# Encoder trunk: weight-block sums moved from the vector engine to accumulating DMAs, and the last norm spread into the last product's own PSUM bank

## Chip, cores and metric

The kernel runs on one core of one Trainium2 chip. The metric is the device time of one execution in microseconds (us). Before the change three runs gave a median of 1677.84 us (1677.39 to 1680.4). Matrix products run on TensorE (PE in the profile), elementwise work on VectorE (DVE) and ScalarE (ACT); GpSimd (POOL) and SyncE (SP) mostly issue DMAs.

## The reference

One layer of an encoder, 1024 positions by 1024 channels, in float32. Only its second part matters here:

```python
merged = jnp.einsum('blkd,blkd->bld', gates, proj)
x = x + g1 * (merged @ w_out[l])
h2 = rmsnorm(x, norm2_g[l]) * (1.0 + sc2) + sh2
f = jnp.square(jax.nn.relu(h2 @ w_ff1[l])) @ w_ff2[l]      # d_ff = 4096
x = x + g2 * f
return rmsnorm(x, final_g)
```

`w_out` is 1024x1024; `w_ff1` (1024x4096) and `w_ff2` (4096x1024) are used as four 1024x1024 blocks each.

## The kernel before

Everything up to `merged` is the first phase and ends near 930 us of the profile; the change touches `phase2` only.

**Products.** `phase2` multiplies nine pairs of 1024x1024 matrices, one per stage. Stage 0 is `w_out` (eight plain products of 512x512 quadrants). Stages 1 to 8 are the four pairs `w_ff1` block, `w_ff2` block, and use a scheme with seven products of quadrant sums instead of eight (`PW`, `PX`, `WSUM`, `XSUM`): the weight operands of a stage are the quadrants 11, 12, 21, 22 and the four sums S1 = 21+22, S2 = S1+11, S3 = 11+21, S4 = S2+12. Each sum exists for two halves h (128 partitions x 1024 float32, 512 KB), so there are 8 stages x 4 sums x 2 halves = 64 of them. Stages with an odd number ("nl", input h2) and an even one ("lin", input f) take the products in different orders; stage 1 has an order of its own, stage 8 the order `EDGE`.

**Granules.** One half of one product is a granule, numbered J = 0 to 127: granules 0 to 15 are stage 0, 16 to 29 stage 1, 30 to 43 stage 2, and so on in steps of 14; 114 to 127 are stage 8. A granule is 24 matmuls of 128x512. Float32 operands are split into a high and a low part: `w2_split(J)` makes `whi` (ACT) and then `wlo` (DVE) from the raw block, `x2_split(J)` makes `xhi` (ACT) and `xlo` (DVE). Weight operands and x operands have four slots each, J modulo 4.

**Order of the work.** The loop over G issues, for each granule: the matmuls of G (with `take(n)` at the start of a product, which reads the previous product out of its four PSUM banks), then `w2_loads(G + 8)` (SP loads raw blocks into eleven raw tiles as these come free), `w2_add(J)` for the sums of the next granules, `w2_split(G + 3)`, the x splits up to G + 3, and `x2_load(G + 3)`. Each engine executes its instructions in that written order and waits in it. In stage 1 the x operands (h2) are also stored to DRAM by POOL (`hop<-xhi`, `hop<-xlo`, two per granule, line 1539), and in all later "nl" stages POOL loads them from there (line 1546). In stage 0 `take_out(i)` updates x and POOL stores it (`xsp`, line 1597).

**Sums.** `w2_add(J)` (line 1447) makes each sum that granule J needs with one DVE addition, `self.add(dst, f[a], f[b])`, once both inputs have their tiles and, where a quadrant's tile is overwritten (`at`), once that quadrant has been split. The loop calls it for J up to G + 4, and in some iterations (lines 1768 to 1770) also for G + 5 to G + 8, after the splits.

**The norm of h2.** `columns(1, ..)` in the middle of granule 17 reduces the squares, `spread(banks[0][0])` in the middle of granule 18 lets PE broadcast the row factors into a PSUM bank, and ACT copies them into `rb` (`nrm<-pm`); `normed` and the splits of granules 20 to 23 follow at the end of granule 18 (line 1719). Bank 0 of that set is free for the spread once ACT has copied the previous product into `u` (`take(0)`).

**The end.** The last product (granules 126 and 127) is computed in two column halves q = 0, 1 of 256. Ahead of it stand `take(54)` (DVE updates, ACT squares), and `scaled` (eight ACT copies); after its first quarter come `spread(banks[0][0])`, which needs a bank that `take(54)` still reads, and `final` (four POOL multiplications by `rb`). `summed()` lets PE add up squares; `take_part(q)` updates x from half q; `rows_part(q)` computes the row factors on DVE (with one ACT square root), `spread_part(q)` broadcasts them, and `last` multiplies and stores the output.

Of the kernel before, what the change touches and what calls it, by code (L numbers as in the profile page):

```python
# [44 lines left out]
class Program:  # L45
# [1401 lines left out]
    def w2_add(self, J):  # L1447


        s, pos, h = self.gran[J]  # L1450
        f = self.wform.get((s, h), {})
        for n, st in enumerate((self.wplan[s][pos] or ((),))[0]):
            if st[0] == "sum" and (J, n) not in self.wdone:
                _, name, a, b, at, freed = st
                if not {a, b, at or name} <= f.keys() or {at, freed} & {self.wplan[s][q][1] for q in range(pos)
                                                                     if (s, q, h) not in self.wsplit}:
                    return False
                self.wdone.add((J, n))
                dst = f[at or name]
                self.add(dst, f[a], f[b])  # L1460
                f[name] = dst
                if freed:
                    self.rawfree.append(f[freed])
        return True
# [83 lines left out]
    def phase2(self):  # L1548
# [50 lines left out]
        def take(n):  # L1599
            s, pos = divmod(n, 7)  # L1600
            s += 1
            kind, order = self.STAGES[s]
            i, set_ = order[pos], banks[n % 2]
            if kind == "lin":
                k, t = {1: (0, 0), 2: (0, 0), 6: (1, 0), 4: (1, 0), 7: (1, 1), 5: (1, 1), 3: (0, 1)}[i]
                for m in range(4):
                    upd(s, k, t, m, set_[m])
                    if s == 8 and i in (6, 2, 5):
                        square(t, k, m)
                for m in range(4 * (s == 8 and i == 5)):  # L1610
                    upd(s, 0, 1, m, set_[m])
                return
            for m in range(4):
                p = set_[m]
                if i == 1:
                    self.act(ub(m), p, ACTF.Copy)
                elif i == 6:
                    self.add(ub(m), ub(m), p)
                    if order == self.NL0:
                        self.add(fb(0, 1, m), fb(0, 1, m), ub(m))  # L1620
                elif i == 2:
                    f = fb(0, 0, m)
                    if order == self.NL0:
                        self.add(f, ub(m), p)
                        self.act(f, f, ACTF.Relu)
                    else:
                        self.act(f, p, ACTF.Relu)
                    self.act(f, f, ACTF.Square)
                elif i == 3 and order == self.NL0:
                    self.act(fb(0, 1, m), p, ACTF.Copy)  # L1630
                elif i == 7 and order == self.NL0:
                    self.add(fb(1, 1, m), ub(m), p)
                elif i == 5 and order == self.NL:
                    self.add(fb(1, 1, m), ub(m), p)
                elif i == 4:
                    f = fb(1, 0, m)
                    self.add(f, ub(m), p)
                    self.stt(f, f, 0.0, f, ALU.min, ALU.mult)
                else:
                    if i in (7, 5):  # L1640
                        f = fb(1, 1, m)
                        self.add(f, f, p)
                        self.act(f, f, ACTF.Relu, scale=-1.0)
                        self.act(f, f, ACTF.Square)
                    if i in (3, 5):
                        f = fb(0, 1, m)
                        self.add(f, ub(m) if i == 3 else f, p)
                        self.stt(f, f, 0.0, f, ALU.max, ALU.mult)
# [15 lines left out]
        def squares():  # L1664
            while late:
                a, sq = late.pop()
                self.add(a, a, sq)
# [27 lines left out]
        def scaled(k, t):  # L1695
            for m in range(4):
                self.act(xb(k, t, m), xb(k, t, m), ACTF.Copy, scale=self.col("fg", 2 * m + k))
# [29 lines left out]
        for G in range(-4, n_g - 2):  # L1727
            if G >= 0:
                s, pos, h = self.gran[G]
                if s == 0:  # L1730
                    if G and G % 4 == 0:
                        take_out(G // 4 - 1)
                    bank, begins, ends, skip = banks[G // 4 % 2], G % 4 == 0, G % 4 == 3, False
                else:
                    n, (kind, order) = 7 * (s - 1) + pos, self.STAGES[s]
                    if h == 0:
                        take(n - 1) if n else take_out(3)
                    i, bank = order[pos], banks[n % 2]
                    skip = pos > 1 and order[pos - 2] == self.GOES_ON[kind].get(i)
                    begins, ends = h == 0 and not skip, h == 1  # L1740
                (whi, wlo), (xhi, xlo) = self.wops[G % 4], self.xop[G % 4]
                for p in range(2):
                    if p:
                        for f in at.get((G, "mid"), ()):
                            f()
                    for m in range(4):
                        o = slice(p * 512 + m * 128, p * 512 + (m + 1) * 128)
                        for c, (w, x) in enumerate(((whi, xhi), (whi, xlo), (wlo, xhi))):
                            self.mm(bank[m], w[:, o], x[:, p, :], start=begins and p == c == 0,
                                    stop=ends and p == 1 and c == 2, skip=skip)  # L1750
                for f in at.get((G, "end"), ()):
                    f()
            squares()
            self.w2_loads(G + 8)
            for J in range(max(G + 1, 0), min(G + 5, n_g)):
                self.w2_add(J)
            for J in range(G + 1, min(G + 5, n_g)):
                if J >= 0 and self.x2_own(J) and not 20 <= J < 24 and self.x2_there(J) <= G:
                    self.x2_add(J)
            if G >= -3:  # L1760
                self.w2_split(G + 3)
            for J in range(G + 1, min(G + 4, n_g)):
                if J >= 0 and self.x2_own(J) and (not 20 <= J < 24 or G >= 19) and self.x2_there(J) <= G:
                    self.x2_split(J)
            if G >= -3:
                self.x2_load(G + 3)
            self.w2_loads(G + 8)
            if 8 <= G < 16 or G > 32 and self.STAGES[self.gran[G][0]][0] == "nl" and self.gran[G][1] > 1:
                for J in range(G + 5, min(G + 9, n_g)):
                    self.w2_add(J)  # L1770


        cuts = (slice(0, 256), slice(256, 512))
# [16 lines left out]
                            start=seen[q] == b == 0, stop=seen[q] == 4, skip=True)  # L1790
                seen[q] += 1

        take(7 * 7 + 5)
        squares()
        scaled(1, 0)
        scaled(0, 0)
        todo += [(q, acc[1][:, cut]) for q, cut in enumerate(cuts)]
        part = (lambda m: banks[1][m][:, low], lambda m: banks[0][1 + m // 2][:, (low, high)[m % 2]])

        def take_part(q):  # L1800
# [5 lines left out]
        def rows_part(q):  # L1806
            rows(sums[q][:, 0:2], diag[:, cuts[q]])
# [9 lines left out]
        for q in range(2):  # L1817
            for h in range(2):
                (whi, wlo), (xhi, xlo) = (o[(n_g - 2 + h) % 4] for o in (self.wops, self.xop))
                for p in range(2):  # L1820
                    for m in range(4):
                        o = slice(p * 512 + m * 128, p * 512 + (m + 1) * 128)
                        for c, (w, x) in enumerate(((whi, xhi), (whi, xlo), (wlo, xhi))):
                            self.mm(part[q](m), w[:, o], x[:, p, cuts[q]], start=h == p == c == 0 and not (q and m % 2),
                                    stop=h == p == 1 and c == 2, skip=q == 1)
                    if (q, h, p) == (0, 0, 0):
                        spread(banks[0][0])
                        final(1, 0)
                        final(0, 0)
                    elif (q, h, p) == (0, 1, 1):  # L1830
                        summed()
                    elif (q, h, p) == (1, 0, 1):
                        summed()
                        rows_part(0)
            if q:
                spread_part(0)
            take_part(q)
# [3 lines left out]
        for _ in range(2):  # L1841
            self.mm(banks[1][0], self.ones, rb)
        summed()
        rows_part(1)
        spread_part(1)
        for _ in first:
            pass
        for _ in second:
            pass

# [69 lines left out]
```

## Time and profile before

| | us |
|---|---|
| median of three runs | 1677.84 |
| profiled execution | 1678.33 |
| its span | 1676.6 |
| PE busy | 1635.8 (98%) |
| DVE busy | 1253.8 (75%) |
| ACT busy | 669.7 (40%) |
| DMA, mean rate | 153 GB/s |

Shares of busy time are means over stages with different limits, so the rows below are taken stretch by stretch. A releaser behind "<-" is what ended an engine's idle time.

### The profile page before, as it was taken

To read this page: it belongs to the slowest core of one execution; us is meant where nothing else is said; L and a number is where in the kernel's file an instruction comes from. 1 tells how busy PE (TensorE), PEld (TensorE's weight loads), DVE (VectorE), ACT (ScalarE), POOL (GpSimd) and SP (SyncE) were. 2 spreads that over 40 slices of the span, in tenths; PEclk is the share of its full clock that TensorE was granted. 3 is DMA by queue.
4 is the path that set the end of the run, shared out by engine and by line. 5 is a ranking of instruction groups with operands and counts; after the bars stand their busy time and mean duration, and the time that the engine had idled before them with its cause. 6 is when DMAs were issued, how large, how long until landed. Compare 5 with 4: busy or idle time off the path is not lost.

```text
span 1676.6 us, 19562 instructions
## 1 busy us (share of the span) xinstructions
PE 1635.8 (98%) x7480; PEld 1350.6 (81%) x7480; DVE 1253.8 (75%) x1912; ACT 669.7 (40%) x876; POOL 74.6 (4%) x130
## 2 busy tenths in 40 slices
PE   6999999999999999999999999999999999999996
PEld 4888878888878888888888888777888888888885
DVE  8889787769877875455666649899559847974896
ACT  5433323554436537552221235643243334323443
POOL 0000000000000000000000001100110021012002
PEclk9999999999999999999999999999999999999998
DMA  8421435533545444054464624661571274157102
GB/s 318 170 88 63 132 107 149 181 136 110 167 145 195 156 170 151 26 188 141 186 240 174 255 97 188 238 233 44 212 274 39 91 252 175 51 171 261 58 1 101
DMA packets 84768, 257.05 MB, mean 153 GB/s; under 512 B 9921, under 2 KB 24385, under 8 KB 83650
## 3 DMA queue, kind: packets, MB, share of 16 engines
q1 hardware_dynamic: 62274, 175.05, 30.8%
q0 software_dynamic: 17792, 67.12, 10.8%
q10 hardware_dynamic: 4608, 13.63, 2.1%
q8 instruction: 59, 0.97, 0.2%
q14 instruction: 35, 0.29, 0.1%
HBM read 199.14 MB, written 54.53 MB: 151 GB/s over the span
## 4 chain that ended last, share of the span: by engine, by line
PE 81%; DVE 11%; issue 3%; ACT 2%; DMA 2%; SPq 1%; DVEq 0%; ACTq 0%
PE pm L91 58%; PE pb L91 22%; DVE xlo L105 2%; DVE wlo L105 2%; DVE xg L122 1%; DVE fr L105 1%; DVE wr L105 1%; DVE fr L122 1%; SPq L149 1%; DMA ada<-ada 1%; DVE s L126 1%; DMA u<-zs 1%; DVE ssacc L105 1%; PE pb L96 0%; DMA lx<-zr 0%
## 5 line engine op out<-in xcount | busy, mean ns | idle before, releaser
L91 PE MATMUL pm<-act,whi 128*128 128x512 f32 x2176 | 673.1, 392 | 2.4 <-ACT act L146 2.4
L91 PEld LDWEIGHTS pm<-act,whi 128*128 128x128 f32 x2176 | 406.1, 188 | 88.3 <-ACT act L146 3.6
L91 PE MATMUL pm<-act,wlo 128*128 128x512 f32 x1088 | 419.8, 389 | 0.0
L146 ACT ACTIVATE whi<-wr 128x1024 fp32r<-128x1024 f32 x124 | 131.0, 1057 | 298.1 <-PE pm L91 128.8
L91 PEld LDWEIGHTS pm<-act,wlo 128*128 128x128 f32 x1088 | 204.4, 188 | 43.0
L105 DVE TENSOR_TENSOR wlo<-wr,whi 128x1024 fp32r<-128x1024 f32 x124 | 151.3, 1221 | 114.1 <-ACT whi L146 114.1
L91 PE MATMUL pb<-xhi,whi 128*128 128x512 f32 (+1 forms) x512 | 200.6, 392 | 5.0 <-DVE fr L105 2.7
L91 PE MATMUL pm<-xlo,whi 128*128 128x512 f32 (+1 forms) x528 | 203.8, 386 | 1.5 <-DVE xlo L105 1.5
L91 PE MATMUL pm<-xhi,whi 128*128 128x512 f32 (+1 forms) x528 | 204.6, 387 | 0.0
L91 PE MATMUL pm<-xhi,wlo 128*128 128x512 f32 (+1 forms) x528 | 203.8, 386 | 0.0
L91 PE MATMUL pb<-xlo,whi 128*128 128x512 f32 (+1 forms) x512 | 199.5, 390 | 0.6 <-DVE xlo L105 0.6
L91 PE MATMUL pb<-xhi,wlo 128*128 128x512 f32 (+1 forms) x512 | 199.2, 389 | 0.0
L146 ACT ACTIVATE whi<-wraw 128x1024 fp32r<-128x1024 f32 x74 | 78.1, 1057 | 102.7 <-PE pm L91 85.6
L91 PEld LDWEIGHTS pb<-xhi,whi 128*128 128x128 f32 x512 | 97.5, 190 | 26.2 <-issue 3.8
L91 PEld LDWEIGHTS pm<-xlo,whi 128*128 128x128 f32 x528 | 99.2, 188 | 21.9 <-DVE xlo L105 1.9
L91 PEld LDWEIGHTS pm<-xhi,whi 128*128 128x128 f32 x528 | 99.2, 188 | 20.1 <-issue 0.2
L91 PEld LDWEIGHTS pm<-xhi,wlo 128*128 128x128 f32 x528 | 99.2, 188 | 20.1
L91 PEld LDWEIGHTS pb<-xlo,whi 128*128 128x128 f32 x512 | 97.5, 190 | 21.2 <-DVE xlo L105 1.0
L91 PEld LDWEIGHTS pb<-xhi,wlo 128*128 128x128 f32 x512 | 97.5, 190 | 19.7
L105 DVE TENSOR_TENSOR wlo<-wraw,whi 128x1024 fp32r<-128x1024 f32 x74 | 90.0, 1218 | 8.0 <-ACT whi L146 7.7
L105 DVE TENSOR_TENSOR wr<-wr,wr 128x1024 f32<-128x1024 f32 x64 | 77.5, 1219 | 0.6
L146 ACT ACTIVATE xhi<-fr 128x1024 fp32r<-128x1024 f32 x54 | 56.6, 1050 | 44.4 <-DVE fr L122 23.3
(265 smaller groups left out, 1908.2 us busy)
## 6 DMA issues: line engine op xcount, KB each, us to landing
wr<-w SPq DMA_DIRECT2D x76, 512.0 KB, 4.5
ada<-ada SPq DMA_DIRECT2D x48, 512.0 KB, 6.4
xhi<-hop POOLq DMA_DIRECT2D x42, 512.0 KB, 3.6
xlo<-hop POOLq DMA_DIRECT2D x42, 512.0 KB, 4.9
wraw<-wgate SPq DMA_DIRECT2D x32, 512.0 KB, 3.9
tg<-tg ACTq DMA_DIRECT2D x24, 512.0 KB, 2.9
tl<-tg SPq DMA_DIRECT2D x24, 512.0 KB, 5.6
wraw<-win SPq DMA_DIRECT2D x20, 512.0 KB, 3.6
```

The source lines that it names most:

```text
L91: self.P.matmul(out=out, lhsT=lhsT, rhs=rhs, start=start, stop=stop, skip_group_check=skip)
L105: self.V.tensor_tensor(out=out, in0=a, in1=b, op=op)
L122: self.V.scalar_tensor_tensor(out=out, in0=a, scalar=s, in1=b, op0=op0, op1=op1, **kw)
L126: self.V.tensor_tensor_scan(out=out, data0=a, data1=b, initial=0.0, op0=ALU.mult, op1=ALU.add)
L146: self.A.activation(out=out, in_=a, func=f, **kw)
L149: (self.S if q == "S" else self.A).dma_start(out=out, in_=a)
```

## The change

The sums of `w2_add` become DMAs issued by POOL. Where the sum overwrites an input, one accumulating DMA adds the other input to it; where it has a tile of its own, a plain DMA copies the first input there and an accumulating DMA adds the second. All of them move 512 KB from SBUF to SBUF. `w2_add` is now called for J up to G + 8 in every iteration, ahead of the splits, and the extra calls after the splits are gone. At the end the spread goes into bank 3 of the last product's own set, after the first three matmuls; `take(54)`, the squares and `scaled` follow it, each `scaled` in front of its `final`; the remaining `last` of half 0 are issued before `rows_part(1)`.

```diff
                 dst = f[at or name]
-                self.add(dst, f[a], f[b])
+                if at is None:
+                    self.G.dma_start(out=dst, in_=f[a])
+                self.G.dma_start(out=dst, in_=f[a if at == b else b], accum_op=ALU.add)
                 f[name] = dst
...
-            for J in range(max(G + 1, 0), min(G + 5, n_g)):
+            for J in range(max(G + 1, 0), min(G + 9, n_g)):
                 self.w2_add(J)
...
-            if 8 <= G < 16 or G > 32 and self.STAGES[self.gran[G][0]][0] == "nl" and self.gran[G][1] > 1:
-                for J in range(G + 5, min(G + 9, n_g)):
-                    self.w2_add(J)
...
-        take(7 * 7 + 5)
-        squares()
-        scaled(1, 0)
-        scaled(0, 0)
-        todo += [(q, acc[1][:, cut]) for q, cut in enumerate(cuts)]
...
                     for m in range(4):
+                        if q == h == p == 0 and m == 1:
+                            spread(banks[1][3])
+                            take(7 * 7 + 5)
+                            squares()
+                            todo += [(q, acc[1][:, cut]) for q, cut in enumerate(cuts)]
+                            for k in (1, 0):
+                                scaled(k, 0)
+                                final(k, 0)
...
-                    if (q, h, p) == (0, 0, 0):
-                        spread(banks[0][0])
-                        final(1, 0)
-                        final(0, 0)
-                    elif (q, h, p) == (0, 1, 1):
+                    if (q, h, p) == (0, 1, 1):
...
         summed()
+        for _ in first:
+            pass
         rows_part(1)
         spread_part(1)
-        for _ in first:
-            pass
```

## Rows read from the trace of the kernel before

**Rows 1.** Windows: us; busy us of PE, PEld, DVE, ACT, POOL; PEclk, DMA share, GB/s.
```profile
1080.00:1130.00 50.00, 49.24 (x218) 40.45 (x216) 49.52 (x59) 21.94 (x25) 4.77 (x9) 1.00 0.69 268
1130.00:1150.00 20.00, 16.98 (x66) 13.56 (x67) 19.90 (x22) 8.03 (x8) 0.00 (x0) 0.91 0.18 53
1150.00:1642.50 492.50, 492.50 (x2181) 408.03 (x2180) 375.67 (x410) 178.84 (x205) 44.23 (x84) 1.00 0.40 137
1642.50:1651.60 9.10, 4.69 (x17) 3.46 (x16) 7.13 (x11) 7.51 (x13) 0.00 (x0) 0.62 0.00 0
```
**Rows 2.** PE's waits in stage 2: us in total, times, longest.
```profile
PE pb L91 <- DVE xg L122: 2.3, 1, 2.3
PE pm L91 <- DVE xlo L105: 1.5, 1, 1.5
```
**Rows 3.** Page, part 5: the sums as a group.
```profile
L105 DVE TENSOR_TENSOR wr<-wr,wr 128x1024 f32<-128x1024 f32 x64 | 77.5, 1219 | 0.6
```
**Rows 4.** DVE timeline of stage 2: start, us, instruction, count.
```profile
1109.14 1.22 DVE L105 TENSOR_TENSOR wr<-wr,wr 128x1024 f32<-128x1024 f32 x1
...
1130.59 2.48 DVE L105 TENSOR_TENSOR wr<-wr,wr 128x1024 f32<-128x1024 f32 x2
```
**Rows 5.** DMA issues in stages 0 and 1: KB each, median us from issue to landing.
```profile
xsp<-xg POOLq DMA_DIRECT2D x1, 1024.0 KB, 4.1
hop<-xhi POOLq DMA_DIRECT2D x1, 512.0 KB, 2.9
```
**Rows 6.** Page, part 6: the x loads, two issued in a row.
```profile
xhi<-hop POOLq DMA_DIRECT2D x42, 512.0 KB, 3.6
xlo<-hop POOLq DMA_DIRECT2D x42, 512.0 KB, 4.9
```
**Rows 7.** DMA issues between 1070 and 1100 us, the busiest stretch.
```profile
hop<-xhi POOLq DMA_DIRECT2D x7, 512.0 KB, 7.4
```
**Rows 8.** Window of stage 1 in which POOL's queue moves nearly all bytes.
```profile
1022.00:1040.00 18.00, 18.00 (x83) 14.89 (x82) 17.19 (x21) 6.78 (x10) 4.25 (x8) 1.00 0.58 231
```
**Rows 9.** POOL timeline, granules 12 and 13.
```profile
1015.48 0.53 POOL L1597 DMA_DIRECT2D xsp<-xg  x1 [27.69 <-DVE xg L122]
1019.05 0.53 POOL L1539 DMA_DIRECT2D hop<-xhi  x1 [3.04 <-ACT xhi L146]
```
**Rows 10.** ACT timeline, granules 13 to 19.
```profile
1017.71 1.04 ACT L146 ACTIVATE xhi<-xg 128x1024 fp32r<-128x1024 f32 x1
...
1039.77 1.05 ACT L146 ACTIVATE whi<-wr 128x1024 fp32r<-128x1024 f32 x1
1040.72 2.04 ACT L146 ACTIVATE u<-pm 128x512 f32<-128x512 f32 x4
1044.71 0.60 ACT L146 ACTIVATE nrm<-pm 128x512 f32<-128x512 f32 x1 [1.95 <-PE pm L91]
...
1054.81 1.04 ACT L146 ACTIVATE whi<-wr 128x1024 fp32r<-128x1024 f32 x1
```
**Rows 11.** PE timeline: the spread in granule 18.
```profile
1043.66 1.02 PE L91 MATMUL pm<-nrm,ones 128*128 128x512 f32 x2
```
**Rows 12.** POOL timeline in stage 3: one x load.
```profile
1233.20 0.53 POOL L1546 DMA_DIRECT2D xhi<-hop  x1 [4.39 <-PE pb L91]
```
**Rows 13.** PE timeline at the end.
```profile
1647.21 2.08 PE L91 MATMUL pm<-nrm,ones 128*128 128x512 f32 x2 [4.41 <-DVE xg L122]
...
1655.31 0.36 PE L91 MATMUL pm<-xhi,whi 128*128 128x256 f32 x1
```
**Rows 14.** DVE timeline at the end.
```profile
1641.77 0.69 DVE L105 TENSOR_TENSOR nrm<-ident,rsq 128x512 f32<-128x512 f32 x1
...
1653.62 1.66 DVE L122 SCALAR_TENSOR_TENSOR xg<-pb,g,xg 128x256 f32<-128x256 f32 x4 [3.89 <-PE pb L91]
...
1666.95 0.16 DVE L118 TENSOR_SCALAR rsq<-pm 128x2 f32<-128x2 f32 x1 [1.23 <-PE pm L91]
```
**Rows 15.** ACT timeline at the end: the eight scalings.
```profile
1646.52 4.99 ACT L146 ACTIVATE xg<-xg,cols 128x512 f32<-128x512 f32 x8
```

## The prediction

> **What bounds the kernel now.** I read the windows first. From 1150 to 1642.5 us PE is busy in every microsecond at full granted clock [rows 1]: nothing that helps DVE or ACT can shorten this stretch, a late operand can only lengthen it. So I looked for the places where PE waits. In stage 2 DVE is busy 49.5 of 50 us and then 19.9 of 20, PE loses 0.76 and 3.02 us there, to two waits of 1.5 and 2.3 us, both ended by DVE [rows 1, 2], and the granted clock falls to 0.91 over the second 20 us. At the end PE waits 4.41 us for DVE [rows 13], and over the 9.1 us from 1642.5 the granted clock is 0.62 [rows 1], between the levels of 1.2 and 2.4 GHz. These two places are what the change can win. The third thing to see is a place without slack: in stage 1 the ACT timeline has, one behind the other, `whi` of granule 20 at 1039.77, the copies into `u`, and the copy of the spread [rows 10]; PE puts the spread into the bank of the first `u` copy at 1043.66 [rows 11].
>
> **The sums leave DVE.** 64 additions of 1.22 us, 77.5 us in all, go [rows 3]. Almost all of it is cover already. In stage 2 it is not: six sums stand between 1109.14 and the pair at 1130.59 [rows 4], 1.14 us each in sequence. By the first wait DVE has done four of them, by the second six: 4.6 and 6.8 us, more than the 1.5 and 3.8 us of PE's backlog. I count both waits (0.76 + 3.02 = 3.8 us) and the slower clock behind them, (1 - 0.91) x 20 = 1.8, of which I take 1.7: **-5.5**. What is late next is an accumulation that lands too late for its split; see below.
>
> **What one DMA costs.** The trace has no accumulating DMA and no copy from SBUF to SBUF. For a copy I take the 2.9 us of a 512 KB store from SBUF on the same queue [rows 5]. POOL's queue moved 231 GB/s at a share of 0.58, so some 400 GB/s at full share [rows 8]: 1.3 us for 512 KB; of two loads issued in a row the second lands 1.3 us later [rows 6], so I let such transfers follow one another. An accumulation has to read its destination as well as its source. Its bounds are 2.9 us, if that costs nothing, and 7.4, the store in the busiest stretch [rows 7]. Its nearest row is the 1024 KB store at 4.1 us [rows 5], which also takes in two blocks: I take 4.1, of which 2.6 are transfer. A POOL DMA that waits starts some 0.3 us after its releaser: `xhi` at 1017.71 lasts 1.04 us, its store issues at 1019.05 [rows 9, 10].
>
> The trace's cheapest price for a block of this size is 2.9 us, and it shows nothing on adding. The Trainium skill (Collectives: The Full Stack, "The bandwidth ceiling: the fold count and why AG ≠ RS ≠ AR") says that a DMA that adds is slower than one that copies, not because of the addition but because two sources are read through one ring, at about half the rate. By that an estimate would be 2.9 + 1.3 = 4.2 us, and the end at 2.9 would be out of reach, with the faster time that follows from it.
>
> **Stage 1 pays.** By the order in which `w2_add` is called, POOL's queue from granule 12 on becomes: the x store; for half 0 copy and add S1, copy and add S2; for half 1 copy and add S1; only then the six operand stores of granules 16 to 18; the last x store; add S4 and S3 of half 0; granule 19's stores; copy and add S2, add S4 and S3 of half 1. Each add waits for its copy, each copy of S2 for the add of S1, and POOL waits in order. On the old time axis: the x store issued at 1015.48 [rows 9] lands at 1019.6, copy S1 behind it at 1020.9, add S1 at 1025.3, copy S2 at 1028.5; add S2 runs to 1032.9 and half 1's copy behind it to 1034.2; its add lands at 1038.6. Behind that the six stores, issued in a burst from 1035, take 6 x 1.3 and end at 1046.4, the x store 2.6 more, add S4 at 1051.6, add S3 at 1054.2. Granule 20 splits S4: its `whi`, at 1039.77 before, starts at 1051.9. ACT's queue holds the `u` copies behind it, so PE's spread waits until 1053.4 instead of 1043.66. The copy of the spread comes 3.0 us behind `whi`'s start, 1054.9 instead of 1044.71 [rows 10]. Meanwhile half 1: copy S2 1057.4, add 1061.8, add S4 1066.2, so `whi` of granule 21 starts at 1066.5 instead of 1054.81 [rows 10]. The rest of that chain (DVE's `wlo`, the norm, the take that PE already waited for) follows it in order: **+11.7**. With 2.9 us for an add the same sums give `whi` of granule 20 at 1047.0 and the chain through the spread decides: +4.4. With 7.4 us granule 21's `whi` starts near 1089.4: +34.6. One microsecond of the add's price is worth seven here.
>
> **Stage 2's own sums.** They meet POOL behind the stores of granule 26, near 1083, while stores take 7.4 us [rows 7]. Even at 13 us each the second S3 lands near 1119; with DVE 4.6 us ahead its split is due near 1121. I cost this at 0 and at +5.5, the gain of stage 2, if it is late.
>
> **The later stages.** In "nl" stages POOL also issues the x loads, and waits for PE most of each granule (4.39 of some 5.4 us, 24 x 0.226) [rows 1, 12]. The chain of sums ahead of such a stage is 4 copies and 3 adds in series, 4 x 3.2 + 3 x 4.4 = 26 us, and starts when a raw tile comes free, 9.5 granules (52 us) before the stage. The first x load is due three granules ahead and takes 4.9 us [rows 6], so its issue may come 47 us after that start. Cover enough; it is gone if an add takes over 11 us. Inside these stages a sum holds POOL back by one landing, against two granules of slack: 0. That is also why the horizon of G + 8 costs nothing by itself.
>
> **The end.** In stage 8 two sums leave DVE right ahead of the factor's last step, which moves from 1641.77 [rows 14] to about 1641.1; it ends at 1641.75. PE has the first three matmuls done, the spread takes 1.0 us at full clock [rows 11] to 1642.8, the ACT copy 0.6; the six matmuls of m = 1, 2 cover it, 0.1 us is left. A 512-column matmul takes 0.226 us (492.5 / 2181 [rows 1]), one of 256 columns about 0.12; the other 45 end at 1648.2. ACT's squares now stand behind the copy, so `take(54)` ends where it did, 1653.62 - 3.89 = 1649.73 [rows 14], and `summed()` waits for it: 1.5 us of PE, then 0.75 for the sums. Half 1 starts at 1650.5, not 1655.31 [rows 13]: -4.8. The eight scalings still end at 1651.5 [rows 15], in time for the squares of half 0. POOL's four multiplications start 3 us earlier and end long before the last store. The moved `last` calls put 8 x 0.4 us of DVE ahead of the factor chain where 4 stood, which fills 1.23 us of waiting [rows 14] and exceeds it by 0.35. **-4.4**.
>
> **Sum.** 11.7 - 5.5 - 4.4 = +1.8 us. The profiled execution took 1678.33, 0.5 above the median, so 1677.84 + 1.8 = **1679.6**. By the skill's 4.2 it would be 1680.3.
>
> **Rivals.**
> *Adding costs a plain store* (2.9 us). For it: rows of 2.9 exist on this queue. Against: a second block must be read. 4.4 - 9.9 = -5.5: 1672.3, faster.
> *Adding is dear*: stage 1's chain, POOL's order of sums ahead of stores, decides alone from 4.4 us per add on (+0.2% and more). For it: nothing in the trace bounds it above, and the burst of stores stands in the same queue. At 5.5 us, 1689; at 7.4 with stage 2's gain lost, 1677.8 + 34.6 - 4.4 = 1708.
> *Stage 2's sums come late*: 1679.6 + 5.5 = 1685. For it: the crowded queue at 1080 to 1100; against: DVE's lead.
> *The burst hides*: if the six stores move beside the adds and not ahead of them, add S4 lands up to 7.8 us earlier: 1672 to 1675.
>
> **Chances.** A measurement here tells about 0.2%, 3.4 us, from no change. The forecast, adds of 3.7 to 4.8 us: 0.40, range 1676 to 1684, of it 0.02 faster, 0.22 same and 0.16 slower. Cheap adds 0.22, faster. Dear adds 0.20, slower. Late sums 0.06, slower. Hidden burst 0.12, faster. Together faster 0.36, same 0.22, slower 0.42. The range, 1668 to 1702, reaches from a cheap add with the burst half hidden to adds of 7.3 us.
>
> **What would show it.** An accumulating DMA of 512 KB lands 4.1 us after issue when nothing is ahead of it. `whi` of granule 20 waits for a DMA, the spread of granule 18 waits for ACT, and PE is idle near 1044 to 1053, not before. PE's two waits between 1120 and 1140 are gone. Half 1 of the last product starts under 2 us behind half 0. PE stays full from stage 3 to stage 7. The prediction is wrong if the adds land much sooner or later, or if PE waits for an x load.

## Result and profile after

The changed kernel takes 1723.84 us (median of four runs, 1722.0 to 1725.58) against 1678.54 for the kernel before on the same chip: ratio 1.0271, interval 1.0259 to 1.0283. It is slower by 45 us, and the forecast of 1679.6 and its range, 1668 to 1702, are both missed.

The loss is laid out by marks that all traces have: the `xsp` store of granule 12 (1015.48 before), the copies `fr<-pm` of stage 1 (1074.85), the first matmul of granule 43, the last of stage 2 (1189.22), the copies `u<-pm` in the third granule of stage 3 (1203.70), the first 256-column matmul (1641.21), and the end of the span. Each column is how much longer the kernel takes from one mark to the next than the profile of before does; the first is how late it reaches stage 1, which no kernel here changes and which lies between -1.1 and +2.8 us. Each row is one execution. `tail_late` has the instructions of the kernel before in stage 2, so its -1.6 there is scatter.

| kernel | ahead | stage 1 | stage 2 | start of stage 3 | rest of 3 to 8 | end | span |
|---|---|---|---|---|---|---|---|
| predicted | 0 | +11.7 | -5.5 | 0 | 0 | -4.4 | +1.8 |
| after | +1.0 | +17.8 | +0.1 | +2.1 | +26.2 | -1.7 | +45.4 |
| own_queue | -0.6 | +15.5 | +2.1 | +6.7 | -1.5 | -1.7 | +20.5 |
| stage1_dve | -1.0 | 0 | -0.5 | +1.9 | +22.1 | -1.7 | +20.8 |
| s3_dve | +1.5 | +14.7 | +0.5 | +1.9 | +0.5 | -0.2 | +19.0 |
| plain | +2.6 | +7.2 | -4.4 | 0 | +15.4 | -0.1 | +20.7 |
| combo | +0.6 | 0 | -4.1 | +4.9 | 0 | -0.3 | +1.1 |
| s2_free | +0.9 | 0 | +3.5 | 0 | 0 | +0.5 | +4.9 |
| tail_only | +0.9 | 0 | 0 | 0 | 0 | +0.5 | +1.4 |
| tail_late | +2.8 | 0 | -1.6 | 0 | 0 | +2.9 | +4.1 |
| tail_dve | -0.2 | 0 | 0 | 0 | 0 | -2.3 | -2.6 |
| both | -1.1 | 0 | -4.2 | +6.8 | 0 | -3.0 | -1.4 |

In the rows below a time in brackets is the idle time ahead of an instruction, with what ended it. First the page of the changed kernel: the new DMA instructions as a group (busy us, mean ns, idle before them), POOL's queue (packets, MB, share of 16 engines), and the issues with the median us to landing.

```profile
L1462 POOL DMA_DIRECT2D wr<-wr x64 | 57.7, 926 | 280.0 <-DMA wr<-wr 161.7
...
q0 software_dynamic: 30464, 113.26, 22.7%
...
wr<-wr POOLq DMA_DIRECT2D x88, 512.0 KB, 6.2
...
xhi<-hop POOLq DMA_DIRECT2D x42, 512.0 KB, 8.6
xlo<-hop POOLq DMA_DIRECT2D x42, 512.0 KB, 9.6
```

DVE's 77.5 us [rows 3] are gone, and POOL stands idle 161.7 us ahead of its additions, waiting for another DMA to land. The x loads, 3.6 and 4.9 us before [rows 6], take 8.6 and 9.6. Windows (columns as in [rows 1]): that of stage 2 (18.8 us later than in [rows 1]), the one from 1170 us to the first 256-column matmul (through the like stretch of [rows 1] PE was busy all the time), and PE's waits from 960 us to the end:

```profile
1098.80:1148.80 50.00, 47.05 (x205) 37.73 (x204) 40.96 (x52) 19.78 (x23) 10.25 (x16) 1.00 0.97 335
...
1170.00:1688.30 518.30, 500.51 (x2165) 411.15 (x2164) 321.51 (x360) 178.42 (x205) 97.57 (x151) 0.98 0.68 198
```

```profile
PE pm L91 <- ACT u L146: 11.8, 1, 11.8
PE pm L91 <- DMA xhi<-hop: 9.4, 3, 5.8
...
PE pb L91 <- DVE nrm L105: 2.5, 1, 2.5
PE pm L91 <- DVE nrm L105: 2.4, 1, 2.4
```

DVE has 9 us to spare in stage 2, and DMA share has gone from 0.69 to 0.97 there. None of the waits of [rows 2] is on top of the list; waits for ACT and for x loads are.

**The price of an addition.** From the chain of waits, in a stretch where little else moves (start, us, what):

```profile
1194.07 2.91 DMA wr<-wr
...
1197.26 5.19 DMA wr<-wr
...
1203.03 2.86 DMA wr<-wr
...
1206.17 5.66 DMA wr<-wr
```

The copies take the 2.9 us I gave them, the additions 5.2 and 5.7, not 4.1.

**Stage 1.** POOL, then ACT, of the changed kernel, where [rows 9, 10] had `hop` stores and `whi` at 1039.77:

```profile
1022.14 0.88 POOL L1462 DMA_DIRECT2D wr<-wr  x1 [4.47 <-DMA wr<-wr]
...
1036.69 0.85 POOL L1462 DMA_DIRECT2D wr<-wr  x1 [4.74 <-DMA wr<-wr]
1037.24 0.84 POOL L1541 DMA_DIRECT2D hop<-xhi  x1
...
1041.73 0.87 POOL L1462 DMA_DIRECT2D wr<-wr  x1 [0.52 <-DMA wr<-wr]
...
1058.07 0.54 POOL L1461 DMA_DIRECT2D wr<-wr  x1 [11.29 <-DMA wr<-wr]
```

```profile
1055.03 1.06 ACT L146 ACTIVATE whi<-wr 128x1024 fp32r<-128x1024 f32 x1 [14.56 <-DMA wr<-wr]
1056.00 2.04 ACT L146 ACTIVATE u<-pm 128x512 f32<-128x512 f32 x4
1058.74 0.60 ACT L146 ACTIVATE nrm<-pm 128x512 f32<-128x512 f32 x1 [0.70 <-PE pm L91]
```

The order on POOL is the predicted one: three additions, then the six stores in one burst (here its first), then S4. `whi` of granule 20 waits for a DMA until 1055.03, PE's spread behind it for the 11.8 us on top of the waits.

**Stage 3.** POOL near the end of the stage, and the PE matmul that waits longest there:

```profile
1255.66 0.53 POOL L1461 DMA_DIRECT2D wr<-wr  x1
1265.01 0.88 POOL L1462 DMA_DIRECT2D wr<-wr  x1 [8.82 <-DMA wr<-wr]
1265.57 0.86 POOL L1548 DMA_DIRECT2D xhi<-hop  x1
1266.10 0.87 POOL L1548 DMA_DIRECT2D xlo<-hop  x1
1266.62 0.87 POOL L1461 DMA_DIRECT2D wr<-wr  x1
1277.44 0.87 POOL L1462 DMA_DIRECT2D wr<-wr  x1 [9.95 <-DMA wr<-wr]
1278.00 0.87 POOL L1548 DMA_DIRECT2D xhi<-hop  x1
```

```profile
1287.37 0.77 PE L91 MATMUL pm<-xhi,whi 128*128 128x512 f32 x1 [5.85 <-DMA xhi<-hop]
```

These are the sums S3 of stage 4, one for each half. Each copy lands 9 to 11 us after its issue, beside the x loads, and POOL waits for it with the next x loads behind it: the pair of a granule goes out at 1265.6 and the next at 1278.0, where PE needs one every 5.4 us. The same stands in stages 5 and 7, 8.0 to 10.0 us each time.

**Stage 2.** POOL, then DVE:

```profile
1131.18 0.87 POOL L1462 DMA_DIRECT2D wr<-wr  x1 [18.89 <-DMA wr<-wr]
1131.75 0.85 POOL L1541 DMA_DIRECT2D hop<-xhi  x1
```

```profile
1142.31 1.23 DVE L105 TENSOR_TENSOR xlo<-sp,xhi 128x1024 fp32r<-128x1024 f32 x1 [8.63 <-DMA hop<-xlo]
```

An addition waits 18.89 us for its copy. The last operand stores wait behind it, the slots they read stay occupied, and DVE, which should have run ahead here, stands still for 8.63 us.

### The profile page after: what moved, and what is told of

It reads as the page before. It is cut to its first block, busy times and chain, and to the rows that moved or that the text cites. A ratio compares the mean times of both kernels' runs of the same rounds, so it can differ in the third digit from the quotient of the medians.

```text
span 1722.0 us, 19727 instructions
## 1 busy us (share of the span) xinstructions
PE 1650.2 (96%) x7480; PEld 1357.6 (79%) x7480; DVE 1184.9 (69%) x1848; ACT 669.2 (39%) x876; POOL 144.7 (8%) x218
## 3 DMA queue, kind: packets, MB, share of 16 engines
q0 software_dynamic: 30464, 113.26, 22.7%
## 5 line engine op out<-in xcount | busy, mean ns | idle before, releaser
L91 PE MATMUL pm<-xhi,whi 128*128 128x512 f32 (+1 forms) x528 | 208.1, 394 | 13.6 <-DMA xhi<-hop 9.4
L91 PEld LDWEIGHTS pm<-xlo,whi 128*128 128x128 f32 x528 | 101.2, 192 | 26.2 <-DMA xlo<-hop 4.1
L1462 POOL DMA_DIRECT2D wr<-wr x64 | 57.7, 926 | 280.0 <-DMA wr<-wr 161.7
```

What stands on the lines that cost most here:

```text
L91: self.P.matmul(out=out, lhsT=lhsT, rhs=rhs, start=start, stop=stop, skip_group_check=skip)
L1462: self.G.dma_start(out=dst, in_=f[a if at == b else b], accum_op=ALU.add)
```

## Experiments

Theory 1 is POOL's written order: stores and x loads stand behind sums that wait for a landing. Theory 2 is traffic: additions load the 16 DMA engines, and everything lands later in whatever order it was issued. In the kernels with a condition, sums for which it fails stay on DVE at their old times:

```diff
-                if at is None:
+                if not (CONDITION):
+                    self.add(dst, f[a], f[b])
+                else:
+                    if at is None:
...
```

**tail_only**: all sums back on DVE at their old times; of the change only the end is left.

```diff
-                if at is None:
-                    self.G.dma_start(out=dst, in_=f[a])
-                self.G.dma_start(out=dst, in_=f[a if at == b else b], accum_op=ALU.add)
+                self.add(dst, f[a], f[b])
...
```

> All 64 sums stay on DVE at their old places; only the end is changed (spread into the last product's own bank, take and scaled behind it, the remaining last calls ahead of the second factor chain). As predicted the end is worth -4.4 us: 1674.1, ratio 0.9974. By the trace of the changed kernel, where the stretch from granule 126 to the end of the span fell from 35.4 to 33.7 us, it is worth -1.7 or less: 1676.8, ratio 0.9990. Rival: the end gains nothing by itself (0.9995 to 1.001), because the factor chain or the moved last calls give it all back.

Measured: 1679.46 us, ratio 1.0004 (0.9995 to 1.0012). The change of the end is worth nothing by itself.

**own_queue**: the operand stores and x loads leave POOL's queue.

```diff
-                self.G.dma_start(out=self.hop[self.STAGES[s][1][pos], h, p], in_=flat(t).bitcast(F32))
+                self.S.dma_start(out=self.hop[self.STAGES[s][1][pos], h, p], in_=flat(t).bitcast(F32))
...
-            self.G.dma_start(out=t.rearrange("p c n -> p (c n)").bitcast(F32), in_=self.hop[self.STAGES[s][1][pos], h, p])
+            self.A.dma_start(out=t.rearrange("p c n -> p (c n)").bitcast(F32), in_=self.hop[self.STAGES[s][1][pos], h, p])
```

> The changed kernel, but the stores of the h2 operands are issued by SP and the x loads by ACT, so POOL's queue holds the sums and the x stores alone. Theory 1 (POOL's written order: stores and x loads stand behind sums that wait for a landing): the 26 us of stages 3 to 7 vanish, stage 1 loses some 8 instead of 18, stage 2 gains about 5: 1685, ratio 1.004. Theory 2 (the sums' traffic on the 16 DMA engines makes everything land late, whoever issues it): 1715 or more, ratio 1.022.

Measured: 1697.33 us, ratio 1.0114 (1.0099 to 1.0129). It lies between the two. The table tells why: with the same bytes moved, the 26.2 us of stages 3 to 8 are gone, so there it was the order, as Theory 1 has it. In stage 1, 15.5 us are left without any operand store in the way. The start of stage 3 is worse: ACT, which now issues the x loads, stands idle for 9.29 us, by the profile for a weight load of SP's queue, ahead of its copy into `u` at 1227.36. That copy is the mark, so the column overstates the loss and the next one understates it: by its matmuls PE is 16.9 us late at granule 43, 20.3 at granule 50 and 22.2 from granule 58 to the end. That was not taken apart.

**stage1_dve**: stage 1's eight sums on DVE.

```diff
+                if not (s != 1):
...
```

> The changed kernel, but the eight sums of stage 1 are DVE additions at their old places. Theory 1 (order): the whi of granules 20 and 21 no longer waits for a DMA, the 17.8 us of stage 1 come back: 1706, ratio 1.017. Theory 2 (traffic, in proportion to the 12 of 88 DMAs that go): 6 us come back: 1718, ratio 1.024.

Measured: 1702.0 us, ratio 1.0147 (1.0132 to 1.0163). Stage 1 loses nothing; most of the rest of the loss stays.

**s3_dve**: S3 of the even stages on DVE. In this kernel S3 of an even stage is taken after S1 has overwritten quadrant 21, so another block is added; the instructions are the same in kind and number.

```diff
+                if not (s % 2 or name != "S3"):
...
```

> The changed kernel, but the S3 sums of stages 2, 4, 6 and 8 (copy and add issued between the operand stores or x loads of the stage before) are DVE additions. Theory 1 (order): PE no longer waits for x loads at the end of stages 3, 5 and 7 and DVE no longer waits for an operand store in stage 2: 20 to 28 us come back, 1696 to 1704, ratio 1.010 to 1.015. Theory 2 (traffic, 16 of 88 DMAs): 8 us come back: 1716, ratio 1.022.

Measured: 1696.29 us, ratio 1.0106 (1.0092 to 1.0119). Behind the start of stage 3 only +0.5 is left: the S3 of the next even stage made the loss of 26.2. The time is inside the range of Theory 1 here, and 4 us below its figure in stage1_dve; both are far from Theory 2. What it does not explain is stage 1 in own_queue, so price and order are separated next.

**plain**: the additions become copies of the same block, all else unchanged.

```diff
-                self.G.dma_start(out=dst, in_=f[a if at == b else b], accum_op=ALU.add)
+                self.G.dma_start(out=dst, in_=f[a if at == b else b])
```

> The changed kernel with each accumulating DMA made a plain copy of the same block: no addition is done, so the sums are left out, and everything else (count, sizes, queue, order, waits) stays. Price of adding: if the loss hangs on what one add costs (5.2 us from issue to landing against 2.9 for a copy, and twice the bytes on the DMA engines), stage 1 loses 2 to 6 us instead of 17.8 and stages 3 to 7 lose under 8 instead of 26: 1684 to 1692 us. Written order: if it is enough that any DMA stands ahead of the stores and x loads in POOL's queue, the same waits come for the copies: stage 1 still over 10, stages 3 to 7 still over 15, in all above 1703 us.

Measured: 1689.8 us, ratio 1.0054 (1.0036 to 1.0073), with runs from 1686.15 to 1699.17; the profiled one is the longest. By the medians, the price of adding carries three quarters of the loss: 10 us are left of 45. The profiled execution, 9.4 us above the median, has 20.7 left, and what the faster ones lose less is not shown. It agrees for stage 1, 7.2 us of 17.8. In stages 3 to 8 it shows 15.4 of 26.2, with copies still waited for 9 us in front of x loads, so in this execution the written order loses there even with cheap DMAs, and the price adds to it. Stage 2 gains 4.4 us, nearly the 5.5 forecast: that gain exists if the sums are cheap. POOL's queue in this kernel:

```profile
q0 software_dynamic: 30464, 113.26, 18.0%
...
wr<-wr POOLq DMA_DIRECT2D x88, 512.0 KB, 3.8
```

22.7% of 1722.0 us less 18.0% of 1697.3 is 85 us, 1.3 us for each of 64 additions: an addition holds the 16 engines about twice as long as a copy (18.0% here against 10.8% of 1676.6 us before is 1.4 us for each of 88), as I had put it. The rest of its 5.2 us is delay, not transfer. The Trainium skill (Collectives: The Full Stack, "The bandwidth ceiling: the fold count and why AG ≠ RS ≠ AR") has the rule, for the reduce step of a collective, that an adding DMA reads two sources at about half the rate. These two shares agree with it; it does not give the landing.

**combo**: both of these on DVE, and S1 of the even stages with them, so that S3 comes ahead of it.

```diff
+                if not (s != 1 and (s % 2 or name not in ("S1", "S3"))):
...
```

> The changed kernel with all sums of stage 1, and S1 and S3 of the even stages, back on DVE at their old times; S2 and S4 of the even stages and all four of the odd stages from 3 on stay DMAs. If the two losses are separate and local (stage 1: the chain of sums in front of granules 20 and 21; later stages: S3 of the next even stage in front of the x loads), both go: start +1.0, stage 2 up to +2.5, end up to +0.5, so 1679 to 1683 us. If a loss that is taken away at one place comes back at the next stage, as a queue that is simply too full would show, 1688 us or more.

Measured: 1678.05 us, ratio 0.9991 (0.9979 to 1.0003), no change that can be measured. The two losses are local: the columns of stage 1 and of the rest of 3 to 8 are 0. 40 of the 64 sums are still DMAs here, and two effects of them cancel. In stage 2, where only S2 and S4 are DMAs, issued from 1125.90 on and so behind the crowded stretch, PE gains 4.1 us of the 5.5 forecast. At the start of stage 3 it loses 4.9. POOL's queue (the first copy of stage 3's sums, its last addition ahead of the x loads, the first x load), then PE at granule 44, the first of stage 3:

```profile
1149.45 0.56 POOL L1466 DMA_DIRECT2D wr<-wr  x1 [13.63 <-DVE wlo L105]
...
1185.18 0.84 POOL L1467 DMA_DIRECT2D wr<-wr  x1 [2.60 <-DMA wr<-wr]
1185.73 0.85 POOL L1553 DMA_DIRECT2D xhi<-hop  x1
```

```profile
1192.74 0.47 PE L91 MATMUL pm<-xhi,whi 128*128 128x512 f32 x1 [1.46 <-DMA xhi<-hop]
1194.78 0.80 PE L91 MATMUL pm<-xlo,whi 128*128 128x512 f32 x1 [1.56 <-DMA xlo<-hop]
```

The first x load goes out 36.3 us after the first copy and takes 7.0. PE is ready 41.8 us after that copy, 1.5 us before the load is there. The granted clock is 0.86 from 1190 to 1202, which adds to the two waits.

**s2_free**: the kernel before with stage 2's eight sums as DMAs, called up to G + 8, and the operand stores on SP.

```diff
+                if not (s == 2):
...
-                self.G.dma_start(out=self.hop[self.STAGES[s][1][pos], h, p], in_=flat(t).bitcast(F32))
+                self.S.dma_start(out=self.hop[self.STAGES[s][1][pos], h, p], in_=flat(t).bitcast(F32))
...
```

> The kernel before, with only the eight sums of stage 2 as DMAs (called up to G + 8), and the operand stores of stage 1 issued by SP so that they do not stand behind the sums; all else, the end too, as before. If freeing DVE of these sums is worth what I took (PE's waits of 1.5 and 2.3 us and the lower clock behind them go): 1672 to 1675 us. If the sums land too late for their splits in the crowded stretch (an add there waited 18.9 us for its copy), or SP's stores now hold the weight loads back: 1678 to 1686 us.

Measured: 1682.74 us, ratio 1.0019 (1.001 to 1.0029). DVE gets ahead as I counted on, but the sums are late. A window, then ACT:

```profile
1080.00:1130.00 50.00, 50.00 (x222) 41.40 (x221) 48.82 (x57) 20.59 (x24) 5.42 (x7) 1.00 1.02 355
```

```profile
1138.03 1.06 ACT L146 ACTIVATE whi<-wr 128x1024 fp32r<-128x1024 f32 x1 [17.87 <-DMA wr<-wr]
```

The 16 engines are full (1.02, against 0.69 before and 0.76 in combo), and a split waits 17.87 us. Here Theory 2 is right. How much SP's stores, which stand ahead of weight loads, add to it was not separated.

**tail_late**: tail_only with the scalings and POOL's multiplications behind `take_part(0)` and the `last` calls in their old order.

```diff
-                            for k in (1, 0):
-                                scaled(k, 0)
-                                final(k, 0)
...
             take_part(q)
+            if not q:
+                for k in (1, 0):
+                    scaled(k, 0)
+                    final(k, 0)
...
```

> The kernel before with the spread moved as in the change, but the eight scalings and POOL's four multiplications issued only behind the updates of half 0, and the moved calls of last put back behind the second factor. If the gain of the end was eaten by POOL's multiplications beside DVE's addition (1.79 instead of 0.68 us) and by the moved last calls: PE's wait ahead of half 1 shrinks from 2.44 to about 1.3 us and the end comes 2 to 3 us earlier, 1675 to 1677 us. If PE's wait at that place lowers its clock whatever its length, and the slow matmuls behind it take the time back: 1678 to 1680 us.

Measured: 1681.61 us, ratio 1.001 (1.0002 to 1.0019). The time is above both ranges. The ratio to the kernel before on this chip (1679.45) would fit the second, but not its reason: PE's wait did shrink to 1.33 us and half 1 ran at full clock. Then came a stall that neither named. POOL, DVE and PE of this kernel:

```profile
1655.14 9.35 POOL L1703 TENSOR_TENSOR xg<-xg,nrm 128x1024 f32<-128x1024 f32 x4 [98.74 <-ACT xg L146]
```

```profile
1659.06 3.15 DVE L105 TENSOR_TENSOR rsq<-rsq 128x2 f32<-128x2 f32 x2
1662.24 2.27 DVE L118 TENSOR_SCALAR rsq<-rsq 128x2 f32<-128x2 f32 x1
```

```profile
1665.22 4.11 PE L91 MATMUL pb<-nrm,ones 128*128 128x256 f32 x6 [4.73 <-DVE nrm L105]
```

DVE operations on two columns, 0.36 us a pair elsewhere, last about as long as one of POOL's multiplications (2.3 us), and PE waits 4.73 us for the factor.

**tail_dve**: as tail_late, but the multiplications go to DVE, three behind `take_part(0)`, one behind the first four `last` calls.

```diff
-                self.G.tensor_tensor(out=x, in0=x, in1=rb.unsqueeze(1).to_broadcast([128, 2, 512]), op=ALU.mult)
+                self.tt(x, x, rb.unsqueeze(1).to_broadcast([128, 2, 512]), ALU.mult)
...
```

> As tail_late (the spread moved, last in its old order), but the four multiplications by rb are done by DVE instead of POOL: three in its idle time ahead of the first factor, one behind the first four last calls. In tail_late the first factor's chain of 128x2 operations took 7 us instead of 2 while POOL multiplied, and PE waited 4.7 us for it. If POOL's multiplication beside DVE is what eats the gain of the end, that wait goes and the end comes 3 us earlier than in the kernel before, less up to 1 us for the DVE work added: 1675.5 to 1677.5 us. If the end is set by something else (the stores of out, PE's clock), it stays at 1679 or above.

Measured: 1675.53 us, ratio 0.9984 (0.9975 to 0.9993), as expected and faster than the kernel before by 0.16%. The factor's operations on DVE and the start of half 1's sums on PE:

```profile
1649.59 0.68 DVE L105 TENSOR_TENSOR nrm<-nrm,nrm 128x512 f32<-128x512 f32 x1
...
1658.20 0.36 DVE L105 TENSOR_TENSOR rsq<-rsq 128x2 f32<-128x2 f32 x2
```

```profile
1650.32 1.08 PE L91 MATMUL pm<-ones,nrm 128*128 128x1 f32 x8 [1.33 <-DVE nrm L105]
```

**both**: combo with this end.

```diff
+                if not (s != 1 and (s % 2 or name not in ("S1", "S3"))):
...
+                self.tt(x, x, rb.unsqueeze(1).to_broadcast([128, 2, 512]), ALU.mult)
...
```

> combo (stage 1's sums and S1, S3 of the even stages on DVE, the other sums DMAs) with the end of tail_dve. If the two parts add up: 1 us under the kernel before for combo's sums, with combo's own end worth nothing, and 2 to 3 us for the end, so 1674 to 1677.5 us, faster than both kernels. If the gain of combo was none and DVE's three multiplications are in its way at the end: 1678.5 us or more.

Measured: 1676.56 us, ratio 0.9988 (0.9974 to 1.0003). The time lies in the first range, but the interval reaches 1. The end keeps its gain (-3.0). Stage 2 gains 4.2 us again, as in combo, and the start of stage 3 takes 6.8: PE waits 1.84 and 1.60 us for the x loads of granule 44, and the granted clock is 0.54 from 1194.3 to 1200. tail_dve, without any accumulating DMA, has the lowest median, but its interval overlaps that of both. A kernel with stage 2's S2 and S4 as DMAs and stage 3's sums on DVE, which these columns point to, was not run.

## Why the prediction was wrong

**Later stages, "a sum holds POOL back by one landing, against two granules of slack: 0": this failed most, 26.2 us.** I set one landing of 2.9 to 4.1 us against 10.9 us. The landing was 9 to 11 us, and two halves came one granule after another, 8.8 + 10.0 us of waiting. s3_dve and own_queue each remove it, one by the sums, one by the order. The copy moves beside the x loads issued just ahead of it and SP's weight loads, at a DMA share of 0.94 (1255.6 to 1265.0); that it lands late for this reason is argued, not tested apart. The same stretch of the kernel before, without any of the new DMAs, was a row to read (DMA share 0.90, 324 GB/s):

```profile
1240.00:1250.00 10.00, 10.00 (x46) 8.29 (x45) 6.70 (x8) 3.05 (x5) 1.53 (x3) 1.00 0.90 324
```

**The other cover, "its issue may come 47 us after that start. Cover enough", gave way at stage 3.** I had the chain start 52 us before the stage, last 26 and the x load take 4.9. In the changed kernel its first copy is issued at 1171.80, 41.9 us before PE is ready for granule 44; the first x load follows 34.9 us later, at 1206.73, and takes 7.5. PE waits 0.54 and 0.99 us there, most of the +2.1 of that column; where PE comes earlier, in combo and both, it costs 4.9 and 6.8. Ahead of stage 5 the chain starts 49.6 us before the stage, and PE does not wait.

**Stage 1, +11.7: the mechanism was right, the price was not.** Order, burst and victims came as written. My own seven microseconds per microsecond of price make 11.7 + 7 x 1.1 = 19.4 of the measured 5.2; it took 17.8. So the rival of dear adds was right on this step, and I had it at 0.20 because I went to the 1 MB store as nearest row: its bytes agree, its delay does not. What the burst of stores, 7.8 us in my sum, costs by itself stays open: own_queue, without it in POOL's queue, still loses 15.5, and there the copy of S2 waits 6.95 us for the first addition, against 4.30 here.

**Stage 2, -5.5: not reached in the changed kernel.** The rival of late sums put stage 2 at 0; it was +0.1 in the changed kernel and +3.5 in s2_free. The step that failed is "I cost this at 0", since it followed the second S3 to its own split only: its addition waited 18.89 us for the copy and held the operand stores behind it, DVE stood still for one of these, and PE, in place of its two old waits, waited 2.9 us for DVE's `fr` and 1.5 for `xlo`. I let DVE's lead decide, while the row that decides is DMA share: 0.69 [rows 1] with 268 GB/s left no room for another 8 sums between 1080 and 1130. Behind that stretch the share falls to 0.18 [rows 1], and there S2 and S4 do fit: combo and both gain 4.1 and 4.2 us, and plain, where all eight are plain copies, 4.4.

**The end, -4.4: -1.7 in the changed kernel, +0.5 in tail_only.** The first stall went as predicted, the spread ran behind the third matmul (in tail_only, with the sums back on DVE, it waits 0.81 us). The step that failed is "`take(54)` ends where it did" and, with it, "POOL's four multiplications start 3 us earlier and end long before the last store". The changed kernel's DVE and PE:

```profile
1696.04 1.80 DVE L105 TENSOR_TENSOR nrm<-nrm,nrm 128x512 f32<-128x512 f32 x1
```

```profile
1697.89 1.05 PE L91 MATMUL pm<-ones,nrm 128*128 128x1 f32 x8 [2.44 <-DVE nrm L105]
```

POOL multiplies from 1694.93, and DVE's addition beside it takes 1.80 us instead of 0.68; another 0.91 is a wait for ACT's squares, which stand behind the copy of the spread. In tail_only the wait of 2.44 us was followed by matmuls at the lower level:

```profile
1652.50:1655.00 2.50, 2.40 (x11) 2.40 (x12) 1.61 (x5) 2.06 (x6) 2.50 (x2) 0.50 0.55 210
```

Half 1's first 24 matmuls then took 5.0 us (1654.33 to 1659.34) where tail_late's took 3.0 at full clock. In the changed kernel they took 4.5 (1698.81 to 1703.26), at a granted clock of 0.54 between 1699.5 and 1703.2; the prediction had no term for a lower clock there. tail_dve, which takes POOL away, has the product's sums start at 1650.32 and ends 2.3 us earlier. It also leaves the moved `last` calls out, so how much of the 2.8 us between the two ends is theirs stays open.

## What to carry to other kernels

A DMA that waits for another DMA is not off the path because its engine is idle: what is written behind it in the same queue waits for the landing under load, not for the quiet one. Before moving work from a full engine to the DMA engines, read the DMA share of the stretch where the gain is expected, and of every stretch in which the new DMAs stand ahead of loads that PE needs, with the landing times there, and price the new DMA from a measurement of one, since bytes alone gave 1.3 of the 2.3 us by which an addition differs from a copy. A total near 0 can be two effects: split it at the stage border before calling a change worthless. When an operation starts earlier beside a critical chain of small operations on another engine, look at whether the two slow each other down.

## What the runs showed of the hardware

An SBUF to SBUF copy of 512 KB landed in 2.9 us and an accumulation in 5.2 to 5.7; POOL was 0.93 us busy with the issue of one on average, and 0.53 with those of plain.

DVE operations with SBUF inputs stretch beside POOL's multiplication: 0.68 us became 1.79 and 1.80, a pair of 0.36 us became 3.15. The updates that read PSUM did not: four of 256 columns took 1.65 us beside it (tail_only) and without it (tail_late). The Trainium skill (SBUF — State Buffer, "Who interferes with whom") has the rule: DVE with two SBUF inputs and a GpSimd instruction that reads SBUF exclude each other, and whoever starts first keeps the port for its whole instruction. The trace agrees for the additions: 1.79 and 1.80 us beside a multiplication against 0.68. The 2.27 us of a TENSOR_SCALAR on two columns, nearly a whole multiplication, is not covered by the rule for two inputs, since it reads one tile; the section names a two-port mode in which such an operation contends too, and no run here shows whether it was in it.

After the same PE wait of 1.33 us the granted clock stayed at 1.00 in tail_late (1651.8 to 1654.3) and was 0.50 in tail_dve from 1651.25 to 1653.75. What decides between the two levels there was not found.
